# Values of a linear-attention head: projected with the tokens as the moving operand, turned by VectorE blocks and a pass through DRAM

## The chip, the cores and the metric

The kernel runs on one core of a Trainium2 chip. The metric is the device time in microseconds; the lower the better. A core has five engines that work from queues of their own and meet through semaphores: TensorE (PE, matmuls), VectorE (DVE), ScalarE (ACT), GpSimd (POOL) and SyncE (SP), which here issues nearly all transfers. TensorE reads SBUF and writes PSUM; of a matmul's two operands one stands still (the weights, loaded first) and one moves through (up to 512 columns). A transfer is issued on an engine's queue in order and then done by 16 shared DMA engines.

## The reference

One decoder layer for 2048 tokens of width 1024 in float32: a mixing stage, a gated MLP with a short convolution, and a final norm. Of the mixing stage the change touches the four heads of gated linear attention (HGRN2, key and value width 128) and the tiles that eight heads of windowed attention turn.

```python
u = rmsnorm(h, norm_mix_w)
hq, hf, hi, hg, att = split(u @ w_in, ...)
f = lb + (1 - lb) * sigmoid(hf);  k = 1 - f;  v = hi
# per head:  S_t = diag(f_t) S_{t-1} + k_t v_t^T,   o_t = S_t^T q_t
o_hg = rmsnorm(o) * silu(hg)
p = softmax(q k^T / 8 in a window of 128 keys, with a sink);  o_att = p @ v_att
h = h + concat(o_hg, o_att) @ w_out
h = h + (silu(conv(rmsnorm(h) @ w_gate)) * (rmsnorm(h) @ w_up)) @ w_down
out = rmsnorm(h)
```

## The kernel before

The tokens are done in two halves of 1024 (`hf`). Each half has a mixing stage, the output product (`out_proj`), the MLP (`gate_up`) and the down product (`down`), which also loads the next half's x and makes its first products.

All large products are float32 products split in two parts: an operand is a high part (rounded, `hi`) and the rest (`lo`), and each product is three matmuls, hi with hi, hi with lo, lo with hi. `prep` loads a weight tile of 128x1024 into a `raw` buffer (three of them, `RAW`), ScalarE casts it to `hi` and VectorE subtracts to get `lo` (two buffers each); the load is at line 198, the cast and the difference at 199 and 200. `unit` (line 203) then makes one product for 128 output rows and 1024 tokens: 8 pieces of the depth, three matmuls each, for two blocks of 512 tokens, so 48 matmuls. The weights stand and the tokens move, and the result has the features in the partitions and the tokens along them. It takes two PSUM banks of the pool `mm`, which has four.

The values of the linear heads are the exception. Their readers want the tokens in the partitions, so `project_v` (line 670) lets the tokens stand and the weights move: for a pair of heads and each of 8 groups of 128 tokens it makes 24 matmuls of 256 columns, and ScalarE scales the result by the tokens' inverse norms, which lie in the partitions (`rs`, line 685). `pu` (line 614) and `po` (line 634) read the values, in chunks of 128 tokens, as the moving operand. Two value tiles (`VB`) serve the four heads in turn.

A head goes through the stages f, q, l, s, p of the generator `hgrn`; a pair of attention heads through qa, sc, pv, pw of `attend`. `ORDER` (line 40) is the order in which these stages are written down, with v0 and v1 for the values of the two pairs, g for the gates and m for the splitting of the result. It gives each instruction a priority; a planner with its own model of the durations then lays out every engine's queue, so the blocks of one stage can lie inside those of another. What is laid out is fixed, and each engine works its queue in that order.

`turned` (line 335) turns a 128x1024 tile: VectorE transposes blocks of 32x32, and 16 transfers of 32 partitions x 1 KB, issued by SP, put the blocks in their places. It is used for the probabilities of three attention pairs in the sc stage (two tiles each, line 444) and for the outputs of three linear heads in the p stage (line 652), so 18 times in all. The tile between the two steps (`turn`) comes from the buffers `pp` or `t4`.

SP's queue carries the weights, x, the turns, and what passes through DRAM. GpSimd makes masks at the start and sets one half of `ST` to zero in the l stage of each head (line 507).

Of the kernel before, what the change touches and what calls it, by code (L numbers as in the profile page):

```python
# [17 lines left out]
P = 128  # L18
D = 1024
# [17 lines left out]
            ("P7", "S3", "T3"), ("P2", "A12", "B21"), ("P4", "A22", "T4")]  # L37
AFTER = {2: 'po'}
UP_AFTER = 'T2'
ORDER = ("f0 q0 l0 qa0 v0 sc0 s0 p0 f1 q1 pv0 pw0 l1 qa1 sc1 f2 s1 p1 q2 pv1 pw1 l2 qa2 v1 sc2 f3 s2 p2 q3 pv2 "  # L40
         "pw2 l3 qa3 sc3 s3 p3 pv3 pw3 g0 g1 m4 m5 m6 g2 m0 m1 g3 m7 m2 m3").split()
LEVELS = [1, 2, 4, 8, 16, 32, 64]
NEG = -1.0e30
UT = 7
# [1 line left out]
VB = 2  # L46
TURNED_PAIRS = 3
TURNED_HEADS = 3


@with_exitstack
def hymba_layer(ctx: ExitStack, tc: tile.TileContext, a: dict, out: bass.AP, rows_out: bass.AP):
# [139 lines left out]
    def prep(src, slots=False, parts=(slice(0, D),)):  # L192

        raw = raw4(None)
        hi, lo = [hp.tile([P, D], F32R, tag="m", name=f"w{t}", bufs=KT) if slots else
                  wp.tile([P, D], F32R, tag=t, name=f"w{t}", bufs=2) for t in ("hi", "lo")]
        for c in parts:
            nc.sync.dma_start(raw[:, c], src[:, c])
            nc.scalar.copy(hi[:, c], raw[:, c])  # L199
            nc.vector.tensor_tensor(lo[:, c], raw[:, c], hi[:, c].bitcast(F32), op=ALU.subtract)  # L200
        return hi, lo
# [130 lines left out]
        v = t[r, :]  # L332
        return bass.AP(v.tensor, v.offset + base, [list(v.ap[0])] + dims)

    def turned(p, tag, bufs, src, dst):

        t = p.tile([P, 4, 8, 32], F32, tag=tag, name="turn", bufs=bufs)
        nc.vector.transpose(t, src.rearrange("p n (c j) -> p c n j", j=32))
        for a in range(4):
            for c in range(4):  # L340
                nc.sync.dma_start(dst[32 * c:32 * c + 32, a], t[32 * a:32 * a + 32, c])

    def rows(kv):
        return slice(kv * HD, (kv + 1) * HD)
# [38 lines left out]
    def attend(hf, j, X, invb, KS, V, VD, mix, p):  # L383
# [9 lines left out]
        for g in range(NB):  # L393
            sc = p.tile([P, 2, 4, P], F32, tag="sc", name="sc", bufs=2)
            gs = slice(g * 512, (g + 1) * 512)
            for kv in range(2):
                r, other = rows(kv), rows(1 - kv)

                qx = p.tile([P, 2, 512], F32R, tag="pp", name="qx", bufs=3)
                qh, ql = qx[:, 0], qx[:, 1]  # L400
                nc.scalar.copy(qh[r], qT[r, gs])
                nc.scalar.copy(qh[other], qT[r, gs])
                nc.vector.tensor_tensor(ql[r], qT[r, gs], qh[r].bitcast(F32), op=ALU.subtract)
                nc.scalar.copy(ql[other], ql[r].bitcast(F32))
                for i0 in (0, 2):
                    pb = ps("at", "psc")
                    first = hf == 0 and g == 0 and i0 == 0
                    for i in range(2):
                        n = g * 4 + i0 + i
                        w0 = 1 if first and i == 0 else 0  # L410
                        o = pb[:, i * 256 + w0 * P:(i + 1) * 256]
                        ks = slice((n + w0) * P, (n + 2) * P)
                        for t, qx in enumerate((qh, ql)):
                            nc.tensor.matmul(o, qx[:, (i0 + i) * P:(i0 + i + 1) * P], KS[:, kv, ks],
                                             start=t == 0, stop=t == 1)
                    pv = pb.rearrange("p (i w k) -> p i w k", i=2, w=2)
                    dst = sc[:, kv, i0:i0 + 2]
                    if first:
                        nc.vector.memset(dst[:, 0], NEG)
                        nc.scalar.copy(dst[:, 1], pv[:, 1, 0])  # L420
                    else:
                        nc.scalar.copy(dst, pv[:, :, 0])
                    nc.vector.copy_predicated(
                        dst, C.own.bitcast(U32).unsqueeze(1).to_broadcast([P, 2, P]), pv[:, :, 1])
            m = p.tile([P, 2, 4], F32, tag="mx", name="m", bufs=2)
            nc.vector.tensor_reduce(m.rearrange("p a b -> p (a b)"),
                                    sc.rearrange("p a b c -> p (a b) c"), axis=AX.X, op=ALU.max)
# [12 lines left out]
            nc.vector.reciprocal(den, den)  # L440
            nc.vector.tensor_tensor(sc, sc, den.unsqueeze(3).to_broadcast([P, 2, 4, P]), op=ALU.mult)
            if j < TURNED_PAIRS:
                pt = p.tile([P, 4, 8, 32], F32, tag="sc", name="pt", bufs=2)
                turned(p, "pp", 3, sc.rearrange("p a b c -> p (a b) c"), pt)
                sc = pt
            scs.append(sc)
        yield
# [37 lines left out]
    def hgrn(hf, h, X, invb, vs, WG, gates, mix, p, fu=None):  # L485
# [112 lines left out]
        v = vs[h]  # L598

        kept = TT if hf + 1 < NH else TT - 1  # L600
        Kn = p.tile([P, TT, P], F32, tag="t4", name="Kn", bufs=2)
        for b in range(NB):
            pk = ps("hg", "pkn")
            n = min(4, kept - 4 * b)
            for i in range(n):
                c = slice((b * 4 + i) * P, (b * 4 + i + 1) * P)
                nc.tensor.transpose(pk[:, i * P:(i + 1) * P], K[:, c], ident)
            nc.scalar.copy(Kn[:, 4 * b:4 * b + n].rearrange("p a b -> p (a b)"), pk[:, 0:n * P])
        SS = p.tile([P, TT, P], F32, tag="SS", name="SS", bufs=1)
        for b in range(NB):  # L610
            pu = ps("hg", "pu")
            for c in range(4 * b, min(4 * b + 4, kept)):
                i = c % 4
                marks["pu"] = nc.tensor.matmul(pu[:, i * P:(i + 1) * P], Kn[:, c], v[:, c], start=True, stop=True)
            for c in range(4 * b, min(4 * b + 4, kept)):
                i = c % 4
                if hf == 0 and c == 0:
# [11 lines left out]
        for b in range(NB):  # L629
            at = [po[b][:, i * P:(i + 1) * P] for i in range(4)]  # L630
            empty = hf == 0 and b == 0
            for i in range(4):
                for k in range(2):
                    marks["po"] = nc.tensor.matmul(at[i][rows(k)], ST[:, k, 4 * b + i], v[:, 4 * b + i],
                                                   start=i == 0, stop=empty and i == 0, skip_group_check=True)
            for i in range(4):
                c = 4 * b + i
# [11 lines left out]
            mix[h] = g  # L649
        nc.vector.tensor_tensor(on, on, rs.unsqueeze(2).to_broadcast([P, TT, P]), op=ALU.mult)  # L650
        if h < TURNED_HEADS:
            turned(p, "t4", 2, on, q.rearrange("p (a c q) -> p a c q", a=4, c=TT))
        for b, bs in halves() if h >= TURNED_HEADS else ():
            pt = ps("hg", "pot")
            for i in range(4):
# [11 lines left out]
            nc.vector.tensor_copy(state[:, h], SS[:, TT - 1])  # L667
        yield

    def project_v(hf, pr, X, rs, p):  # L670

        v = [p.tile([P, TT, P], F32, tag="v", name="v", bufs=VB) for _ in range(2)]
        parts = [prep(a["w_v"][pr, s]) for s in range(2)]
        for tt in range(TT):
            o = ps("mm", "pvv")
            t = slice(tt * P, (tt + 1) * P)
            for kt in range(KT):
                hi, lo = parts[kt // 4]
                xh, xl = X[kt]
                c = slice((kt % 4) * 256, (kt % 4 + 1) * 256)  # L680
                nc.tensor.matmul(o[:, 0:256], xh[:, t], hi[:, c], start=kt == 0, stop=False)  # L681
                nc.tensor.matmul(o[:, 0:256], xl[:, t], hi[:, c], start=False, stop=False)  # L682
                nc.tensor.matmul(o[:, 0:256], xh[:, t], lo[:, c], start=False, stop=kt == KT - 1)  # L683
            for i in range(2):
                nc.scalar.activation(v[i][:, tt], o[:, i * P:(i + 1) * P], AF.Identity, scale=rs[:, tt:tt + 1])
        return v

    def split_into(h, l, src, eng=None):
# [465 lines left out]
    for hf in range(NH):  # L1154
        X, kv, invb, rs, f0 = nxt
        with ExitStack() as st:
# [7 lines left out]
            for name in ORDER:  # L1164
# [7 lines left out]
                elif stage == "w":  # L1172
                    WG[n] = prep(a["w_g"][n])
                elif stage == "v":
                    vs += project_v(hf, n, X, rs, p)
                else:
                    M[n] = split(mix[n], C.hgw if n < TURNED_HEADS else None)
            for n in (7, 3):
# [8 lines left out]
def _layout(i):  # L1187
# [3 lines left out]
    def cols(w, idx):  # L1191
# [10 lines left out]
    rows = [ar(P) + h * P for h in range(4)]  # L1202
    rows += [512 + np.concatenate([j * HD + ar(HD), (j + 4) * HD + ar(HD)]) for j in range(4)]
    w_out = i["w_out"][0][np.concatenate(rows)]
    w_v = np.stack([cols(w_in, 1024 + pr * 256 + ar(256)).reshape(P, 2, D).transpose(1, 0, 2) for pr in range(2)])
    conv = np.concatenate([i["conv_w"][0], i["conv_b"]], 0)
    d = {
        "xT": x.T.reshape(KT, P, S),
# [1 line left out]
        "norm_mix_w": i["norm_mix_w"][0].reshape(KT, P).T,  # L1210
        "w_q": np.stack([cols(w_in, h * P + ar(P)) for h in range(4)]),
        "w_f": np.stack([cols(w_in, 512 + h * P + ar(P)) for h in range(4)]),
        "w_v": w_v,
        "w_g": np.stack([cols(w_in, 1536 + h * P + ar(P)) for h in range(4)]),
        "w_att": np.stack([cols(w_in, c) for c in att]),
        "b_attn": np.stack([b[c - att0] for c in att], 1),
# [37 lines left out]
```

## Time and profile before

| | us |
|---|---|
| three runs, median (lowest to highest) | 2129.19 (2128.93 to 2129.20) |
| the profiled run | 2129.44 |
| its span, first to last instruction | 2127.7 |
| ScalarE busy | 1050.0 |
| GpSimd busy | 16.9 |

The span is the time from the first to the last instruction in the profile; what the profiled run has beyond it, 1.7 us, lies around it. The mixing stages take about 50 to 345 us and 1085 to 1400 us of the span; between them lie the output product, the MLP and the down product of the first half. Busy times are sums over the records of an engine. Matmuls are pipelined, and the ends of their records are modelled, so that the records of neighbours overlap.

### The profile page before, as it was taken

The numbers are of one execution on the slowest core, as the hardware profiler recorded it, in microseconds if no ns is written. First come the engines' busy times: TensorE is split into PE (matmuls) and PEld (weight loads), VectorE is DVE, ScalarE is ACT, GpSimd is POOL, SyncE is SP. The second block draws the span as 40 slices with busy tenths as digits, with TensorE's granted clock in tenths as the row PEclk, the third lists the DMA queues.
The fourth block names the chain that finished last, engine by engine and source line by source line (L and its number), as shares of the span: only waits on it lengthen the run. The fifth ranks groups of instructions, "written<-read, shape, count | busy, mean of one in ns | idle before, by whom it ended". The sixth has DMA issues, their size and how long they took to land.

```text
span 2127.7 us, 30275 instructions
## 1 busy us (share of the span) xinstructions
PE 2113.7 (99%) x11575; PEld 1763.0 (83%) x11575; DVE 1632.4 (77%) x2427; ACT 1050.0 (49%) x1855; POOL 16.9 (1%) x43
## 2 busy tenths in 40 slices
PE   8999999999999999999999999999999999999998
PEld 6988888888888888888889898888888888888887
DVE  6587786798887878785865776867988788887765
ACT  5455645564444445335635456555544444453353
POOL 2000000000000000000000000000000000000000
PEclk9999999999999999999999999999999999999999
DMA  4121213413232335964641212242223323259644
GB/s 162 42 59 45 68 52 102 136 59 121 91 124 92 98 116 168 379 235 150 216 143 40 61 38 64 60 146 97 80 99 103 110 90 124 94 194 403 228 149 134
DMA packets 105810, 264.34 MB, mean 124 GB/s; under 512 B 15808, under 2 KB 28608, under 8 KB 105664
## 3 DMA queue, kind: packets, MB, share of 16 engines
q1 hardware_dynamic: 105232, 262.14, 36.6%
q8 instruction: 91, 1.49, 0.3%
q14 instruction: 55, 0.45, 0.1%
q10 hardware_dynamic: 432, 0.27, 0.0%
HBM read 195.56 MB, written 57.34 MB: 119 GB/s over the span
## 4 chain that ended last, share of the span: by engine, by line
PE 97%; DVE 2%; DMA 1%; ACT 0%; issue 0%; SPq 0%; ACTq 0%; DVEq 0%
PE X L818 7%; PE X L816 7%; PE X L817 7%; PE pop L218 7%; PE hq L218 4%; PE q L218 4%; PE g L218 4%; PE f L218 4%; PE Y L817 4%; PE Y L818 4%; PE Y L816 4%; PE pdx L1004 3%; PE pdx L1003 3%; PE pdx L1005 3%; PE pdy L1004 3%; PE pdy L1003 3%
## 5 line engine op out<-in xcount | busy, mean ns | idle before, releaser
L689 ACT CAST whi<-raw 128x1024 fp32r<-128x1024 f32 x88 | 92.7, 1053 | 115.1 <-PE X L817 73.1
L816 PE MATMUL X<-T,whi 128*128 128x512 f32 x352 | 136.9, 389 | 0.0
L817 PE MATMUL X<-T,whi 128*128 128x512 f32 x352 | 136.9, 389 | 0.0
L818 PE MATMUL X<-T,wlo 128*128 128x512 f32 x352 | 136.9, 389 | 0.0
L887 DVE SCALAR_TENSOR_TENSOR y<-ga,cw,y 128x1024 f32<-128x1024 f32 x88 | 112.5, 1279 | 25.9 <-ACT y L885 25.9
L822 ACT COPY u<-X 128x512 f32<-128x512 f32 x88 | 51.5, 585 | 122.8 <-PE X L818 122.6
L690 DVE TENSOR_TENSOR wlo<-raw,whi 128x1024 fp32r<-128x1024 f32 x88 | 107.2, 1218 | 4.4 <-ACT whi L689 4.4
L199 ACT CAST whi<-raw 128x1024 fp32r<-128x1024 f32 x58 | 60.6, 1050 | 89.9 <-PE pop L218 36.7
L690 DVE TENSOR_TENSOR xld<-raw,xhd 128x1024 fp32r<-128x1024 f32 x72 | 80.9, 1131 | 18.3 <-ACT xhd L689 18.2
L689 ACT CAST xhd<-raw 128x1024 fp32r<-128x1024 f32 x72 | 70.0, 978 | 37.6 <-DMA raw<-act0T 12.0
L218 PE MATMUL pop<-XL,whi 128*128 128x512 f32 x256 | 82.8, 390 | 0.0
L218 PE MATMUL pop<-XH,wlo 128*128 128x512 f32 x256 | 82.6, 390 | 0.0
L218 PE MATMUL pop<-XH,whi 128*128 128x512 f32 x256 | 82.5, 391 | 0.0
L200 DVE TENSOR_TENSOR wlo<-raw,whi 128x1024 fp32r<-128x1024 f32 x58 | 70.5, 1217 | 10.4 <-ACT whi L199 10.1
L818 PEld LDWEIGHTS X<-T,wlo 128*128 128x128 f32 x352 | 66.1, 188 | 13.8
L817 PEld LDWEIGHTS X<-T,whi 128*128 128x128 f32 x352 | 66.1, 188 | 13.7
L816 PEld LDWEIGHTS X<-T,whi 128*128 128x128 f32 x352 | 66.0, 188 | 13.7
L682 PE MATMUL pvv<-whi,XL 128*128 128x256 f32 x256 | 72.7, 285 | 0.0
L681 PE MATMUL pvv<-whi,XH 128*128 128x256 f32 x256 | 72.6, 285 | 0.0
L683 PE MATMUL pvv<-wlo,XH 128*128 128x256 f32 x256 | 72.4, 287 | 0.0
L818 PE MATMUL X<-B,wlo 128*128 128x512 f32 x176 | 68.7, 390 | 0.8 <-DVE wlo L690 0.8
L817 PE MATMUL X<-T,Sh 128*128 128x512 f32 x176 | 68.6, 390 | 0.5 <-DVE T L690 0.5
(388 smaller groups left out, 6287.9 us busy)
## 6 DMA issues: line engine op xcount, KB each, us to landing
wr<-in_w_down SPq DMA_DIRECT2D x90, 512.0 KB, 5.6
raw<-in_w_gate SPq DMA_DIRECT2D x44, 512.0 KB, 3.6
raw<-in_w_up SPq DMA_DIRECT2D x44, 512.0 KB, 3.6
raw<-act0T SPq DMA_DIRECT2D x20, 512.0 KB, 5.6
raw<-act1T SPq DMA_DIRECT2D x20, 512.0 KB, 5.9
act0B<-y SPq DMA_DIRECT2D x33, 256.0 KB, 2.4
act1B<-y SPq DMA_DIRECT2D x33, 256.0 KB, 2.4
raw<-in_w_out SPq DMA_DIRECT2D x16, 512.0 KB, 3.7
```

The source lines that it names most:

```text
L218: nc.tensor.matmul(o[b], w, x[:, bs], start=f, stop=l)
L681: nc.tensor.matmul(o[:, 0:256], xh[:, t], hi[:, c], start=kt == 0, stop=False)
L682: nc.tensor.matmul(o[:, 0:256], xl[:, t], hi[:, c], start=False, stop=False)
L683: nc.tensor.matmul(o[:, 0:256], xh[:, t], lo[:, c], start=False, stop=kt == KT - 1)
L689: nc.scalar.copy(h, src)
L690: return (eng or nc.vector).tensor_tensor(l, src, h.bitcast(F32), op=ALU.subtract)
L816: nc.tensor.matmul(o, wh[:, ws], xh, start=i == 0 and not more, stop=False, skip_group_check=more)
L817: nc.tensor.matmul(o, wh[:, ws], xl, start=False, stop=False, skip_group_check=more)
L818: nc.tensor.matmul(o, wl[:, ws], xh, start=False, stop=i == 3, skip_group_check=more)
L887: nc.vector.scalar_tensor_tensor(y, g[:, w:w + HALF], C.cw[:, ft, w:w + 1], y, op0=ALU.mult, op1=ALU.add)
L1003: nc.tensor.matmul(o, wh[:, i, c], ah[:, i, cols], start=f, stop=False, skip_group_check=more)
L1004: nc.tensor.matmul(o, wh[:, i, c], al[:, i, cols], start=False, stop=False, skip_group_check=more)
```

## The change

Four edits, in one:

- The values are projected per head by `unit`, like every other product: weights stand, 512 tokens move, 48 matmuls. The weight layout is per head. The result, with the features in the partitions, is turned by `turned` into a value tile, and ScalarE scales it there, chunk by chunk. The stages v0 and v1 become v0 to v3, v0 and v1 where v0 was and v2 and v3 where v1 was.
- `turned` takes a list of sources, so that it can transpose two PSUM banks of 128x512. In place of 16 transfers from SBUF to SBUF there are five: one stores the tile of transposed blocks to DRAM (four tiles there, `DB`), and four load it back, each for 32 partitions. This holds for the 18 turns that there were and for the eight new ones.
- The value tile is laid out so that a chunk of 128 tokens' values is four runs of 32; `pu` and `po` read it so.
- `prep` issues its load on GpSimd's queue and not on SP's. That is 58 loads: all weights of the mixing stage and of the output product.

A branch for turning the keys in the same way is there too; with `TURNED_KEYS` at 0 it makes nothing.

```diff
-ORDER = ("f0 q0 l0 qa0 v0 sc0 s0 p0 f1 q1 pv0 pw0 l1 qa1 sc1 f2 s1 p1 q2 pv1 pw1 l2 qa2 v1 sc2 f3 s2 p2 q3 pv2 "
-         "pw2 l3 qa3 sc3 s3 p3 pv3 pw3 g0 g1 m4 m5 m6 g2 m0 m1 g3 m7 m2 m3").split()
+ORDER = ("f0 q0 l0 qa0 v0 v1 sc0 s0 p0 f1 q1 pv0 pw0 l1 qa1 sc1 f2 s1 p1 q2 pv1 pw1 l2 qa2 v2 v3 sc2 f3 s2 p2 q3 pv2 pw2 l3 qa3 sc3 s3 p3 pv3 pw3 g0 g1 m4 m5 m6 g2 m0 m1 g3 m7 m2 m3").split()
...
+TURNED_KEYS = 0
+DB = 4
...
         for c in parts:
-            nc.sync.dma_start(raw[:, c], src[:, c])
+            nc.gpsimd.dma_start(raw[:, c], src[:, c])
             nc.scalar.copy(hi[:, c], raw[:, c])
...
-    def turned(p, tag, bufs, src, dst):
+    def turned(p, tag, bufs, src, dst, strided=False):
 
         t = p.tile([P, 4, 8, 32], F32, tag=tag, name="turn", bufs=bufs)
-        nc.vector.transpose(t, src.rearrange("p n (c j) -> p c n j", j=32))
-        for a in range(4):
-            for c in range(4):
-                nc.sync.dma_start(dst[32 * c:32 * c + 32, a], t[32 * a:32 * a + 32, c])
+        tv = t.rearrange("p c n i -> p c (n i)").rearrange("p c (i n) -> p c n i", n=8) if strided else t
+        for i, s in enumerate(src):
+            n = 8 // len(src)
+            nc.vector.transpose(tv[:, :, i * n:(i + 1) * n], s.rearrange("p (n c j) -> p c n j", n=n, j=32))
+        d = dp.tile([P, 4, 256], F32, tag="turned", name="turned", bufs=DB)
+        nc.sync.dma_start(d.rearrange("p c x -> p (c x)"), flat(t))
+        for c in range(4):
+            nc.sync.dma_start(dst[32 * c:32 * c + 32].rearrange("p a b c -> p a (b c)"),
+                              d[:, c].rearrange("(a j) x -> j a x", a=4))
...
-                marks["pu"] = nc.tensor.matmul(pu[:, i * P:(i + 1) * P], Kn[:, c], v[:, c], start=True, stop=True)
+                marks["pu"] = nc.tensor.matmul(pu[:, i * P:(i + 1) * P], Kn[:, c], v[:, :, c], start=True, stop=True)
...
-    def project_v(hf, pr, X, rs, p):
-
-        v = [p.tile([P, TT, P], F32, tag="v", name="v", bufs=VB) for _ in range(2)]
-        parts = [prep(a["w_v"][pr, s]) for s in range(2)]
-        for tt in range(TT):
-            o = ps("mm", "pvv")
-            t = slice(tt * P, (tt + 1) * P)
-            for kt in range(KT):
-                hi, lo = parts[kt // 4]
-                xh, xl = X[kt]
-                c = slice((kt % 4) * 256, (kt % 4 + 1) * 256)
-                nc.tensor.matmul(o[:, 0:256], xh[:, t], hi[:, c], start=kt == 0, stop=False)
-                nc.tensor.matmul(o[:, 0:256], xl[:, t], hi[:, c], start=False, stop=False)
-                nc.tensor.matmul(o[:, 0:256], xh[:, t], lo[:, c], start=False, stop=kt == KT - 1)
-            for i in range(2):
-                nc.scalar.activation(v[i][:, tt], o[:, i * P:(i + 1) * P], AF.Identity, scale=rs[:, tt:tt + 1])
+    def project_v(h, X, rs, p):
+
+        o = unit(a["w_v"][h], X, "vT")
+        v = p.tile([P, 4, TT, 32], F32, tag="v", name="v", bufs=VB)
+        turned(p, "pp", 3, o, v)
+        for c in range(TT):
+            nc.scalar.activation(v[:, :, c], v[:, :, c], AF.Identity, scale=rs[:, c:c + 1])
         return v
...
-                    vs += project_v(hf, n, X, rs, p)
+                    vs.append(project_v(n, X, rs, p))
```

More of the change, by code (lines that the diff above doesn't have):

```diff
@@ L333, in across, with flat @@
         return bass.AP(v.tensor, v.offset + base, [list(v.ap[0])] + dims)
-    def turned(p, tag, bufs, src, dst):
+    def flat(t):
+        return t.rearrange("p a b c -> p (a b c)")
+    def turned(p, tag, bufs, src, dst, strided=False):
         t = p.tile([P, 4, 8, 32], F32, tag=tag, name="turn", bufs=bufs)
-        nc.vector.transpose(t, src.rearrange("p n (c j) -> p c n j", j=32))
-        for a in range(4):
-            for c in range(4):
-                nc.sync.dma_start(dst[32 * c:32 * c + 32, a], t[32 * a:32 * a + 32, c])
+        tv = t.rearrange("p c n i -> p c (n i)").rearrange("p c (i n) -> p c n i", n=8) if strided else t
[7 more added lines that the diff above has]
+                              d[:, c].rearrange("(a j) x -> j a x", a=4))
     def rows(kv):
@@ L443, in attend @@
                 pt = p.tile([P, 4, 8, 32], F32, tag="sc", name="pt", bufs=2)
-                turned(p, "pp", 3, sc.rearrange("p a b c -> p (a b) c"), pt)
+                turned(p, "pp", 3, [sc.rearrange("p a b c -> p (a b c)")], pt)
                 sc = pt
@@ L600, in hgrn @@
         kept = TT if hf + 1 < NH else TT - 1
-        Kn = p.tile([P, TT, P], F32, tag="t4", name="Kn", bufs=2)
-        for b in range(NB):
+        if h < TURNED_KEYS:
+            Kt = p.tile([P, 4, 32, TT], F32, tag="t4", name="Kt", bufs=2)
+            turned(p, "t4", 2, [K], Kt, True)
+            Kn = Kt.rearrange("p a i n -> p n (a i)")
+        else:
+            Kn = p.tile([P, TT, P], F32, tag="t4", name="Kn", bufs=2)
+        for b in range(NB) if h >= TURNED_KEYS else ():
             pk = ps("hg", "pkn")
@@ L633, in hgrn @@
                 for k in range(2):
-                    marks["po"] = nc.tensor.matmul(at[i][rows(k)], ST[:, k, 4 * b + i], v[:, 4 * b + i],
+                    marks["po"] = nc.tensor.matmul(at[i][rows(k)], ST[:, k, 4 * b + i], v[:, :, 4 * b + i],
                                                    start=i == 0, stop=empty and i == 0, skip_group_check=True)
@@ L651, in hgrn @@
         if h < TURNED_HEADS:
-            turned(p, "t4", 2, on, q.rearrange("p (a c q) -> p a c q", a=4, c=TT))
+            turned(p, "t4", 2, [on.rearrange("p c t -> p (c t)")], q.rearrange("p (a c q) -> p a c q", a=4, c=TT))
         for b, bs in halves() if h >= TURNED_HEADS else ():
@@ L1204, in _layout @@
     w_out = i["w_out"][0][np.concatenate(rows)]
-    w_v = np.stack([cols(w_in, 1024 + pr * 256 + ar(256)).reshape(P, 2, D).transpose(1, 0, 2) for pr in range(2)])
     conv = np.concatenate([i["conv_w"][0], i["conv_b"]], 0)
@@ L1212, in _layout @@
         "w_f": np.stack([cols(w_in, 512 + h * P + ar(P)) for h in range(4)]),
-        "w_v": w_v,
+        "w_v": np.stack([cols(w_in, 1024 + h * P + ar(P)) for h in range(4)]),
         "w_g": np.stack([cols(w_in, 1536 + h * P + ar(P)) for h in range(4)]),
```

## The prediction

> **What bounds the kernel now.** I read the page first, then the waits of TensorE, then TensorE's order of time. From the page (busy time and share, then the chain that ended last by engine):
>
> ```profile
> span 2127.7 us, 30275 instructions
> ...
> PE 2113.7 (99%) x11575; PEld 1763.0 (83%) x11575; DVE 1632.4 (77%) x2427; ACT 1050.0 (49%) x1855; POOL 16.9 (1%) x43
> ...
> PE 97%; DVE 2%; DMA 1%; ACT 0%; issue 0%; SPq 0%; ACTq 0%; DVEq 0%
> ```
>
> TensorE is busy for 2113.7 of 2127.7 us and carries 97% of the chain. What it still waits for is in its waits (total, times, longest) and in the windows (span, then busy time by engine):
>
> ```profile
> PE kv L218 <- ACT XH L232: 5.5, 1, 5.5
> ...
> 50.00:345.00 295.00, 295.00 (x2390) 252.50 (x2390) 220.70 (x414) 165.65 (x427) 0.52 (x1) 1.00 0.20 59
> 345.00:430.00 85.00, 85.00 (x402) 70.55 (x399) 55.26 (x91) 42.17 (x72) 0.00 (x0) 1.00 0.35 115
> 1085.00:1400.00 315.00, 315.00 (x2453) 268.68 (x2453) 228.54 (x418) 172.14 (x426) 2.09 (x4) 1.00 0.22 66
> ```
>
> The 5.5 us are the start. In the mixing stage of both halves (50 to 345 and 1085 to 1400 us), where the change lies, TensorE is busy without a gap and its clock is 1.00. VectorE is busy there for 75% and 73%. So a wait that ends elsewhere, a faster turn or a freer queue is worth nothing: only fewer or cheaper matmuls shorten this stage, and only a new gap on TensorE lengthens it.
>
> **The value products.** The groups by line (count, busy, mean ns) invite a wrong sum:
>
> ```profile
> L682 PE MATMUL pvv<-whi,XL 128*128 128x256 f32 x256 | 72.7, 285 | 0.0
> L218 PE MATMUL hq<-XL,whi 128*128 128x512 f32 x128 | 42.7, 393 | 0.0
> ```
>
> Three such groups make 768 matmuls of 256 columns; the change makes 384 of 512 columns of them (4 heads, 2 halves, 48 each), the form of hq. By the means that is 768 x 285 ns = 219 us against 384 x 393 ns = 151 us, a gain of 68. But a busy time is no cost here, since the records overlap. The cost is the distance from start to start, in TensorE's timeline:
>
> ```profile
> 79.02 0.39 PE L683 MATMUL pvv<-wlo,XH 128*128 128x256 f32 x1
> 79.24 0.28 PE L681 MATMUL pvv<-whi,XH 128*128 128x256 f32 x1
> ...
> 82.12 0.28 PE L681 MATMUL pvv<-whi,XH 128*128 128x256 f32 x1
> 82.33 0.39 PE L558 MATMUL plev<-Q,G 128*64 128x64 f32 x6
> ```
>
> ```profile
> 45.23 0.39 PE L218 MATMUL hq<-XH,wlo 128*128 128x512 f32 x1
> ...
> 50.69 0.39 PE L218 MATMUL hq<-XH,wlo 128*128 128x512 f32 x1
> ```
>
> From 79.24 to 82.12 lie 24 steps: 120 ns a matmul. From 45.23 to 50.69 lie 24 steps: 227.5 ns. Each pair of heads in each half therefore costs 192 x 0.120 = 23.04 us now and 96 x 0.2275 = 21.84 us after. The difference of 1.20 us arises four times: **-4.8 us**. It is one fourteenth of what the busy times promise.
>
> What two half-width matmuls cost more than one whole is 12.5 ns. The Trainium skill, TensorE: Matmul & The Clock Gate, section "Wait — 56ns, not 53.3ns?", puts a matmul of N columns at N / 2.4 GHz plus about 2.5 ns once the clock is up; by that the sum would be an estimated -1.0 us. The two measured distances differ from it, and I go by them.
>
> A second price stands in the same rows: where a block of other matmuls cuts into a run, the step into it is 0.21 us (82.12 to 82.33) and the step out 0.22 (79.02 to 79.24) instead of 0.12, some 0.2 us for each cut. The planner makes TensorE's order anew; ten cuts more or fewer in a half are 2 us. I take none, and keep both signs.
>
> The products that read the values (pu, po) now take them in four runs of 32 instead of 128 in a row. The trace has both kinds on one line:
>
> ```profile
> L471 PE MATMUL poT<-pt,V 128*64 128x128 f32 x180 | 17.9, 275 | 0.0
> L471 PE MATMUL poT<-pw,V 128*64 128x128 f32 x60 | 6.0, 278 | 0.0
> ```
>
> pt is read in such runs, pw in a row: no difference, so 0 us.
>
> **The new path of the values.** After each product come two VectorE block turns of 128x512 out of PSUM, one store to DRAM, a wait of SP for it, four loads, and eight scalings on ScalarE (eight per head before too). The trace has no turn out of PSUM and no such store and reload. The nearest rows:
>
> ```profile
> L338 DVE STREAM_TRANSPOSE turn<-sc x12: 1234/1239/1245, 116.1 to 1331.2; 128x1024 f32<-128x1024 f32 x12
> ...
> L741 DVE TENSOR_TENSOR h<-h,pop 128x512 f32<-128x512 f32 x16 | 10.3, 681 | 14.7 <-PE pop L218 14.7
> ...
> L685 ACT ACTIVATE v<-pvv,y x64: 344/360/369, 76.4 to 1277.6; 128x128 f32<-128x128 f32 x64
> ...
> keep<-h SPq DMA_DIRECT2D x32, 256.0 KB, 2.1
> h<-keep SPq DMA_DIRECT2D x16, 512.0 KB, 8.9
> ...
> act0T<-T SPq DMA_DIRECT2D x22, 256.0 KB, 3.1
> ...
> KS<-kcarry SPq DMA_DIRECT2D x1, 128.0 KB, 3.6
> ```
>
> A turn of half width is 0.62 (half of 1.239) to 0.68 us (L741 reads PSUM); I take 0.68, so 1.4 for two. VectorE gains 16 of them, 11 us in 610, under the TensorE stream that covers it at 75%. The store of 512 KB lies between 2.1 and 8.9; I take 3.1, the slowest store shown. Four issues are 4 x 0.63 = 2.5 (a sixteenth of the 10.08 us below, each), the last landing 1.8 to 3.6, taken at 3.6. Scaling is 8 x 0.36 = 2.9, as before. The chain is **13.5 us**, with ends 10.5 and 19.3. What covers it for head 0, whose values are wanted first:
>
> ```profile
> 97.01 0.28 PE L683 MATMUL pvv<-wlo,XH 128*128 128x256 f32 x1
> 97.13 1.10 PE L414 MATMUL psc<-KS,qx 128*128 128x128 f32 x8
> ...
> 103.98 0.38 PE L614 MATMUL pu<-v,Kn 128*128 128x128 f32 x2
> ...
> 188.31 0.28 PE L681 MATMUL pvv<-whi,XH 128*128 128x256 f32 x1
> ...
> 248.13 1.50 PE L614 MATMUL pu<-v,Kn 128*128 128x128 f32 x12
> ```
>
> After v0's last matmul TensorE has v1 (48 x 0.2275 = 10.9 us), then today's work from 97.0 to 104.0 (7.0): 17.9 us. So 0 us, with 4.4 to spare. Heads 1 to 3 have more: pvv of heads 2 and 3 starts at 188.3, and head 2's pu at 248.1.
>
> **The other turns.** Eighteen turns of probabilities and outputs lose 16 issues each for one store and four loads:
>
> ```profile
> 117.34 10.08 SPq L341 DMA_DIRECT2D pt<-turn  x16
> ...
> pt<-turn SPq DMA_DIRECT2D x192, 32.0 KB, 1.8
> ```
>
> Sixteen issues take 10.1 us, then 1.8 to land: 11.9. The new way is 3.1 + 2.5 + 3.6 = 9.2 (6.4 to 15.0). TensorE waits for none of them, so 0 us either way. SP now waits inside each turn for its store; behind it stand the next turn, the loads of h and the stores of keep, for which TensorE doesn't wait either.
>
> **The weight loads on GpSimd's queue.** 58 loads leave SP, where they waited long for their buffers and were stuck among turns:
>
> ```profile
> SPq L198 <- DVE wlo L200: 255.1, 31, 25.9
> ...
> 47.56 0.33 SPq L198 DMA_DIRECT2D raw<-in_w_f  x1
> ...
> 95.77 1.05 ACT L199 CAST whi<-raw 128x1024 fp32r<-128x1024 f32 x1 [0.69 <-PE pvv L682]
> ```
>
> A load issued at 47.6 is first touched at 95.8, and the cast waits for TensorE to free its buffer, not for the load. So 0 us. The trace has no load issued by GpSimd: between the 3.6 us of SP's w_f loads and 8.9 (h<-keep) I take the former, and 5 us more would vanish in that slack. Two joints remain. GpSimd's queue also holds the memsets of ST:
>
> ```profile
> POOL ST L507 <- DMA pt<-turn: 484.0, 2, 246.1
> ...
> 7.73 5.58 POOL L118 TENSOR_SCALAR_AFFINE_SELECT lmask<-lmask 128x64 f32<-128x64 f32 x10
> ...
> 19.39 0.33 SPq L198 DMA_DIRECT2D raw<-in_w_f  x1
> ...
> 2.00:4.00 2.00, 0.00 (x0) 0.00 (x0) 0.00 (x0) 0.73 (x2) 2.00 (x7) 1.00 0.93 267
> ...
> 10.00:12.00 2.00, 1.99 (x7) 1.09 (x6) 0.72 (x1) 1.91 (x3) 2.00 (x6) 1.00 1.02 412
> ```
>
> The memset that waits 246 us has nothing behind it now; after the change weights stand before and behind it, and lag only as far as the planner misjudges it. And at the start the DMA engines are full (share 0.93 to 1.02): if w_f goes out before the masks, at 13.3 us, and not at 19.4, its 512 KB at 267 to 412 GB/s put 1.3 to 2.0 us before the tiles of x. I take 0 for both.
>
> **Sum:** 2129.4 (the profiled run) - 4.8 = 2124.6; against the median of 2129.2, **2124.4 us**.
>
> **Rivals.**
> 1. The order gets smoother: 10 to 20 cuts fewer, 2 to 4 us: 2120.5 to 2122.5. For it: turns end sooner, so the small blocks come in one piece. Against: their number is the same.
> 2. The gain is given back at the joints: w_f in the first 16 us (2.0), more cuts (2 to 4), or a late weight. 2126.5 to 2133. This holds also the case that a column costs the same in both widths in the long run and nothing is saved: 2129.2, 4 in 100 by itself, against two plain rows. The clock page of the Trainium skill, weighed above, comes near that case.
> 3. Slower: head 0's values come late. SP takes turns one after another, and each now holds it for 3.1 + 2.5 = 5.6 us. With the store at its upper end and one other turn ahead the chain is 19.3 + 5.6 = 24.9 us; less 17.9, TensorE stands 7.0 us in each half: 2124.4 + 14.0 = 2138. It decides from a chain of 17.9 on, and is slower by 0.2% from 22.4. Against it: the nearest turn, pt at 117, follows the values by 20 us.
> 4. A load on GpSimd's queue is held while VectorE works, so that casts hold ScalarE up. With VectorE busy 75% a load of 3.6 us would take 14; three buffers then still give one in under 5 us, and a unit takes 10.9. Only a first load of a stage could be late, some 10 us in each half: 2144.
>
> The group of a VectorE operation with two inputs, beside the turn with one above:
>
> ```profile
> L200 DVE TENSOR_TENSOR wlo<-raw,whi 128x1024 fp32r<-128x1024 f32 x58 | 70.5, 1217 | 10.4 <-ACT whi L199 10.1
> ```
>
> The Trainium skill, SBUF — State Buffer, section "SBUF: two separate sides", warns of this hold for VectorE operations that use two ports for one stream. The trace doesn't show such a mode: 128x1024 takes 1.24 us with one input and 1.22 with two.
>
> **How the numbers follow.** Forecast 0.52 (2123 to 2126.5), rival 1 0.14, rival 2 0.22, rivals 3 and 4 together 0.12 (0.09 and 0.03). A measurement tells 0.2%, here 4.3 us, from no change; that line, 2124.9, runs through the forecast: 0.36 of it counts as faster, 0.16 as the same. Faster 0.36 + 0.14 = 0.50, same 0.16 + 0.22 = 0.38, slower 0.12. The range from 2120.5 to 2132 leaves out rivals 3 and 4 and the edge of 2.
>
> **What would show it.** Right: 384 vT matmuls at 227 ns from start to start, TensorE without a gap in both mixing stages, head 0's pu waiting for nothing. Wrong: a TensorE wait whose releaser is ScalarE's scaling of v or a turned tile (rival 3), a whi cast that waits for raw (rival 4), a start that reaches 16 us of kv work later (rival 2).

## The result

| | us |
|---|---|
| kernel before, four runs | 2129.19 (2128.93 to 2129.60) |
| changed kernel, four runs | 2142.76 (2140.80 to 2146.35) |
| ratio | 1.0065, 95% interval 1.0048 to 1.0083 |
| profiled run of the changed kernel, its span | 2143.43, 2141.7 |

The change makes the kernel 13.6 us slower, where 4.8 us faster was forecast; the time lies above the range. The page of the changed kernel (span; busy time by engine; the chain that ended last):

```profile
span 2141.7 us, 29401 instructions
...
PE 2115.2 (99%) x11191; PEld 1742.8 (81%) x11191; DVE 1639.2 (77%) x2443; ACT 1049.6 (49%) x1855; POOL 48.1 (2%) x101
...
PE 91%; DVE 4%; DMA 2%; ACT 1%; issue 1%; SPq 0%; DVEq 0%; ACTq 0%
```

TensorE's share of the chain falls from 97% to 91%: other engines now set its pace in places. Which, is in its waits (total, times, longest):

```profile
PE poT L481 <- DMA pt<-turned: 9.1, 4, 2.6
PE kv L219 <- ACT XH L233: 6.0, 2, 5.6
PE psc L424 <- DVE sc L433: 1.4, 1, 1.4
```

The second row is the start, as before. The first is new: matmuls that wait for probabilities on their way through DRAM. Among the signs of being wrong that the prediction lists, this one appeared, a TensorE wait for a turned tile; but the tile holds probabilities, not head 0's values. The windows over the two mixing stages, and over three of the places (span, then busy time by engine, TensorE's clock near the end):

```profile
50.00:345.00 295.00, 292.74 (x2176) 239.68 (x2174) 220.39 (x420) 163.74 (x417) 12.16 (x23) 1.00 0.29 89
1085.00:1400.00 315.00, 305.20 (x2195) 249.86 (x2195) 228.36 (x424) 168.87 (x422) 13.23 (x25) 0.99 0.29 87
...
220.00:225.00 5.00, 2.92 (x48) 2.38 (x44) 2.26 (x3) 0.58 (x1) 0.00 (x0) 1.00 0.74 151
...
1280.00:1285.00 5.00, 2.51 (x40) 2.06 (x42) 4.87 (x8) 0.71 (x2) 0.53 (x1) 0.82 0.77 238
1285.00:1290.00 5.00, 5.00 (x40) 4.37 (x37) 4.84 (x10) 1.72 (x3) 0.00 (x0) 0.84 1.06 296
1345.00:1350.00 5.00, 2.44 (x31) 1.81 (x30) 0.56 (x1) 1.82 (x3) 0.00 (x0) 1.00 0.87 255
1350.00:1355.00 5.00, 4.94 (x40) 3.84 (x42) 3.71 (x5) 1.23 (x2) 0.00 (x0) 0.66 0.38 108
```

Both stages were gapless at a clock of 1.00. Now TensorE stands for 2.3 and 9.8 us in them, and behind the second and third of the holes shown the clock is down (0.66 to 0.84); behind the first it stays at 1.00. The first place, in the timelines of VectorE and of SP (start, duration, what, and in brackets the idle time ahead and its releaser):

```profile
213.13 1.25 DVE L346 STREAM_TRANSPOSE turn<-sc 128x1024 f32<-128x1024 f32 x1
...
217.04 0.69 DVE L574 TENSOR_TENSOR K<-K,F 128x512 f32<-128x512 f32 x1
222.70 1.23 DVE L463 TENSOR_TENSOR po<-pt,ownT 128x1024 f32<-128x1024 f32 x1 [4.97 <-DMA pt<-turned]
```

```profile
214.40 1.01 SPq L348 DMA_DIRECT2D turned<-turn  x2
217.64 1.75 SPq L350 DMA_DIRECT2D pt<-turned  x4
```

The turn ends at 214.38, the store goes out at once, SP waits for it until 217.6, and the tile is there at 222.7, 8.3 us after the turn. But the reader of the tile, po<-pt, is laid out only 3.4 us of work behind the turn, so VectorE stands for 4.97 us with all its later work behind it.

The same turn and reader in VectorE's timeline of the kernel before:

```profile
208.57 1.24 DVE L338 STREAM_TRANSPOSE turn<-sc 128x1024 f32<-128x1024 f32 x1
...
222.35 1.23 DVE L453 TENSOR_TENSOR po<-pt,ownT 128x1024 f32<-128x1024 f32 x1
```

There 12.5 us lay between (222.35 less 209.81), and VectorE didn't wait for the tile. There are six places of this kind, the second block of 512 tokens of each turned pair (its second half, in what follows): without the wait for the tile, turn and reader lay 10.2 to 14.6 us apart before and lie 3.4 to 8.4 us apart now.

The second place, in the second half of the tokens, has a further side. In the timelines of TensorE and VectorE:

```profile
1277.02 0.61 PE L219 MATMUL vT<-XH,wlo 128*128 128x512 f32 x2
...
1282.89 0.49 PE L481 MATMUL poT<-pt,V 128*64 128x128 f32 x4 [1.94 <-DMA pt<-turned]
...
1287.27 0.50 PE L219 MATMUL f<-XH,whi 128*128 128x512 f32 x1
```

```profile
1285.60 2.51 DVE L346 STREAM_TRANSPOSE turn<-vT 128x512 f32<-128x512 f32 x4
```

The wait is again for pt. But between the last product of v3 (1277.6) and the first of head 3's f lie 9.6 us in which no large product fills such waits, and TensorE is idle for 2.7 us in all. f takes the banks of the values, and these are turned only from 1285.6 on. In the first half of the tokens f follows v3 at once.

### The profile page after: what moved, and what is told of

The parts are those of the page before. It is cut to its first block, busy times and chain, and to the rows that moved or that the text cites. A ratio compares the mean times of both kernels' runs of the same rounds, so it can differ in the third digit from the quotient of the medians.

```text
span 2141.7 us, 29401 instructions
## 1 busy us (share of the span) xinstructions
PE 2115.2 (99%) x11191; PEld 1742.8 (81%) x11191; DVE 1639.2 (77%) x2443; ACT 1049.6 (49%) x1855; POOL 48.1 (2%) x101
## 4 chain that ended last, share of the span: by engine, by line
PE 91%; DVE 4%; DMA 2%; ACT 1%; issue 1%; SPq 0%; DVEq 0%; ACTq 0%
PE pop L219 7%; PE X L824 7%; PE X L823 7%; PE X L822 7%; PE hq L219 4%; PE g L219 4%; PE Y L824 4%; PE Y L823 4%; PE Y L822 4%; PE q L219 4%; PE pdx L1011 3%; PE pdx L1010 3%; PE pdx L1009 3%; PE f L219 3%; PE pdy L1010 3%; PE pdy L1011 3%
## 5 line engine op out<-in xcount | busy, mean ns | idle before, releaser
L433 DVE COPY_PREDICATED sc<-own,psc 128x256 f32<-128x256 uint32 x64 | 27.5, 448 | 55.3 <-ACT sc L432 42.3
L823 PE MATMUL X<-T,Sh 128*128 128x512 f32 x176 | 68.6, 390 | 0.6 <-DVE T L696 0.6
L822 PE MATMUL X<-B,whi 128*128 128x512 f32 x176 | 68.7, 390 | 0.0
L822 PE MATMUL X<-T,Sh 128*128 128x512 f32 x176 | 68.7, 390 | 0.0
```

Of the source, the lines that this page charges most:

```text
L822: nc.tensor.matmul(o, wh[:, ws], xh, start=i == 0 and not more, stop=False, skip_group_check=more)
L823: nc.tensor.matmul(o, wh[:, ws], xl, start=False, stop=False, skip_group_check=more)
```

## The experiments

Eighteen kernels. In the tables, "time" is the median, and the ratio is to the kernel before in the same session (2129.1 to 2129.4).

### Taking the change apart

| kernel | what it is | time | ratio, 95% |
|---|---|---|---|
| undo_dram | changed kernel, all 26 turns by 16 transfers | 2151.90 | 1.0106 (1.0091 to 1.0121) |
| undo_queue | changed kernel, weight loads on SP's queue | 2137.08 | 1.0038 (1.0026 to 1.0051) |
| only_dram | kernel before, its 18 turns through DRAM | 2133.23 | 1.0018 (1.0009 to 1.0028) |
| only_values | kernel before, values by the new product, turned by 16 transfers | 2150.33 | 1.0099 (1.0084 to 1.0114) |

undo_dram puts the old transfers back into `turned`; only_dram does the reverse in the kernel before; only_values takes `project_v`, `ORDER` and the readers from the change, with this loop; undo_queue moves the weight loads back to SP's queue, where only_values has them too:

```diff
-        d = dp.tile([P, 4, 256], F32, tag="turned", name="turned", bufs=DB)
-        nc.sync.dma_start(d.rearrange("p c x -> p (c x)"), flat(t))
-        for c in range(4):
-            nc.sync.dma_start(...)
+        for a in range(4):
+            for c in range(4):
+                nc.sync.dma_start(dst[32 * c:32 * c + 32, a], t[32 * a:32 * a + 32, c])
...
-            nc.gpsimd.dma_start(raw[:, c], src[:, c])
+            nc.sync.dma_start(raw[:, c], src[:, c])
```

> The changed kernel with all 26 turns done by 16 transfers inside SBUF again; values by 512-column products and weights on GpSimd's queue stay. Theory A (the store and reload is the loss: TensorE and VectorE are laid out to read a turned tile sooner than its 8.3 us are over): the loss goes and the 4.8 us of the products show, 2123 to 2127 us. Theory B (the new path of the values is the loss, however they are turned): 2138 to 2146. Theory C (GpSimd's queue is the loss): 2138 to 2146.

> The changed kernel with the weight loads on SP's queue again; all else stays. Theory A: 2140 to 2146 us, perhaps some more, since the weights stand among the turns again. Theory B: 2138 to 2146. Theory C: 2123 to 2128.

> The kernel before with one edit: its 18 turns pass through DRAM. Values and weight queue are as before. Theory A: most of the 18.4 us between the sum (2124.4) and the measurement (2142.8) shows, 2138 to 2148 us, with TensorE waiting for pt tiles. Theory B and theory C: 2128 to 2131.

> The kernel before with one edit: values by 512-column products, turned by 16 transfers; weights on SP's queue. Theory A: 2123 to 2127 us, the gain of the products alone. Theory B: 2138 to 2146. Theory C: 2123 to 2128. SP then issues 128 transfers of 0.63 us more than before, 80 us in all, so that weights behind them can be late: up to 2132 under any theory.

Theory A, that the way through DRAM is the loss, falls: without it the kernel is 9 us slower still, and alone it costs 3.9. C, that the queue is the loss, explains 5.7 of the 13.6 us. The values cost most (B): 21 us with the old transfers. Each of the four times lies outside the range of the theory that it comes nearest to, so the theories had the direction at best, not the size. The profile of only_values shows where. Its windows, from the end of the products of v3 to the start of head 3's f:

```profile
220.00:225.00 5.00, 3.87 (x50) 2.91 (x49) 4.91 (x9) 1.63 (x2) 0.00 (x0) 1.00 0.40 132
225.00:230.00 5.00, 1.82 (x48) 1.55 (x48) 3.52 (x7) 1.46 (x4) 0.00 (x0) 0.71 0.20 48
230.00:235.00 5.00, 3.93 (x24) 3.19 (x26) 2.55 (x4) 1.17 (x2) 0.00 (x0) 0.50 0.44 125
235.00:240.00 5.00, 5.00 (x33) 4.16 (x30) 1.87 (x3) 2.34 (x4) 0.00 (x0) 0.77 0.17 40
```

TensorE is idle for 5.4 us of the first 15, and its clock falls to 0.50. In that stretch it has only small blocks until f starts, and of its five waits four end with VectorE.

### The values: banks, work or order

| kernel | what it is | time | ratio, 95% |
|---|---|---|---|
| no_turn | only_values without the turn of the values: ScalarE scales them straight from PSUM, so that their readers get them untransposed | 2129.51 | 1.0002 (0.9992 to 1.0011) |
| f_turn | changed kernel, the values' turn tile in the buffers of f instead of pp | 2140.02 | 1.0050 (1.0035 to 1.0065) |
| v3_later | changed kernel, v3 behind f3 in `ORDER` | 2143.95 | 1.0064 (1.0047 to 1.0081) |
| only_queue | kernel before, weight loads on GpSimd's queue | 2129.39 | 1.0000 (0.9991 to 1.0009) |

The edits of f_turn, v3_later and no_turn, in this order:

```diff
-        turned(p, "pp", 3, o, v)
+        turned(p, "f", 2, o, v)
...
-... qa2 v2 v3 sc2 f3 s2 ...
+... qa2 v2 sc2 f3 v3 s2 ...
...
-            nc.scalar.activation(v[:, :, c], v[:, :, c], AF.Identity, scale=rs[:, c:c + 1])
+            nc.scalar.activation(v[:, :, c], oc, AF.Identity, scale=rs[:, c:c + 1])
```

> The kernel with the values alone changed (512-column products, SP's weight queue, 16-transfer turns elsewhere), and the turn of the values left out: ScalarE scales them straight out of PSUM into the value tile, so that the values aren't transposed. Theory B1 (the loss is that v2's and v3's four PSUM banks are held until VectorE turns them, which waits for a turn buffer, so that head 3's f can't begin): the banks are free at once and the products' gain is all that is left, 2123 to 2126 us. Theory B3 (the 512-column products aren't cheaper as they lie in this kernel): 2129 us or more. Theory B2 (the turn of the values costs through the work it gives VectorE and SP, wherever that lies): 2123 to 2126 too.

> The changed kernel with one word altered: the values' turn tile takes a buffer of tag f (two of the same size) and not one of pp, which the probabilities hold. Theory B1: the turn of v2 and v3 no longer waits for the probabilities, the gap after them shrinks, 2128 to 2138 us; f buffers are used by head 3's f, so some of the wait may come back there. Theory B2: 2140 to 2146, as the changed kernel.

> The changed kernel with v3 written after f3 in the order, and not behind v2. Theory B1: v2 and f3 have a pair of banks each, TensorE has wide products while the turns run, 2128 to 2137 us. Theory B2: 2140 to 2146, since the same work is done on VectorE and SP.

> The kernel before with one edit: the weight loads on GpSimd's queue. With the changed kernel the queue was worth +5.7 us (2142.8 against 2137.1). Theory C1 (loads issued by GpSimd cost by themselves, by a later landing or a busier memory): 2133 to 2136 us. Theory C2 (they cost only through another order of the work around the late turns): 2128 to 2131.

The queue alone costs nothing. Without the turn 20.8 us go, so the loss hangs on the turn, not on the product. no_turn is still no faster than the kernel before, which is what B3 (the products aren't cheaper as they lie here) expected. But its windows have 3.7 us of holes at 345 to 360 us, where poT waits 1.9 us for pw and po 1.4 for m, and a clock of 0.66 in the last 5 of these; so this run can't tell B3 from a gain that another place gave back. By their times f_turn and v3_later speak for B2. f_turn's trace says more: v2 is turned within 1 and 5 us of the end of its product, the hole between v3 and f is gone in both halves of the tokens, and the kernel is 2.7 us faster than the changed one; yet other holes remain (3.4 and 6.7 us of idle TensorE in the two stages). So the buffer has a part, and not the largest in this kernel.

### The reader of the probabilities

| kernel | what it is | time | ratio, 95% |
|---|---|---|---|
| g1_16 | changed kernel, turns of each pair's second half by 16 transfers | 2144.16 | 1.0071 (1.0056 to 1.0086) |
| g1_16_sp | the same, weight loads on SP's queue | 2144.80 | 1.0072 (1.0055 to 1.0088) |
| dram_for_v_sp | kernel before, values by the new product and through DRAM, other turns by 16 transfers | 2145.58 | 1.0076 (1.0061 to 1.0091) |
| dram_queue | kernel before, 18 turns through DRAM, weight loads on GpSimd's queue | 2134.88 | 1.0027 (1.0017 to 1.0037) |

```diff
-                turned(p, "pp", 3, [sc.rearrange("p a b c -> p (a b c)")], pt)
+                turned(p, "pp", 3, [sc.rearrange("p a b c -> p (a b c)")], pt, direct=g == 1)
```

> The changed kernel, but the turns of the second half of each attention pair's probabilities (6 of the 26 turns) go from SBUF to SBUF by 16 transfers again. Theory L: the loss comes from the one reader that stands closest behind its turn. In the kernel before VectorE's product po<-pt of a pair's second half started 11.5 to 14.6 us after the end of its turn (10.2 to 14.6 of them filled with laid-out work); in the changed kernel only 3.4 to 8.4 us of work are laid between, and the data takes 7.3 to 11.0 us, so VectorE stands 15.0 us in 4 places and TensorE 9.1 us behind it, with its clock down afterwards. Then with 16 transfers the work between is back at 10 us or more, TensorE's waits for a turned pt fall from 9.1 to under 1 us, and the time falls from 2142.8 to 2129 to 2134. Theory M: the eight new turns of the values load VectorE's and SP's queues and their PSUM banks are held, whichever way other turns go: 2138 or more, with other waits of TensorE in place of those for pt.

> As the run before, with the weight loads on SP's queue again. Theory L: the queue matters only through where the reader of pt comes to stand; with that taken away both queues give the same within 2 us: 2128 to 2134. Theory M: 2135 or more (the changed kernel with SP's queue took 2137.1).

> The kernel before with the values by the new product and turned through DRAM; the 18 other turns by 16 transfers, the weights on SP's queue. Theory L: no wait for pt, so the gain of the products (4.8 us by the distance from start to start) shows, less some small joints: 2125 to 2130. Theory M: the values' new path costs by itself, 2135 or more; with the values turned by 16 transfers it was 2150.3.

> The kernel before with the 18 turns through DRAM and the weights on GpSimd's queue, the values as before. Turns through DRAM alone took 2133.2, the queue alone 2129.4. Theory L: the same wait for pt as with the DRAM turns alone, shifted by where the planner lays it: 2131 to 2136. If the queue by itself makes transfers through DRAM later (it added 5.7 us beside the values): 2138 to 2140.

This theory, L, falls as the only cause. In g1_16 turn and reader lie 9.5 us or more apart again, its TensorE waits for a turn of probabilities no longer than 0.8 us, and it is no faster: the holes are in another place. Between v3's products and f its TensorE is idle for 5.5 us in each half of the tokens, where the changed kernel has none and 2.7. dram_for_v_sp shows that place bare, in TensorE's timeline and in VectorE's:

```profile
219.15 0.62 PE L219 MATMUL vT<-XH,wlo 128*128 128x512 f32 x2
...
221.27 0.64 PE L573 MATMUL plev<-Q,G 128*64 128x64 f32 x16
225.16 0.69 PE L573 MATMUL plev<-Q,G 128*64 128x64 f32 x16 [3.25 <-DVE Q L580]
227.39 1.12 PE L573 MATMUL plev<-Q,G 128*64 128x64 f32 x16 [1.55 <-DVE Q L580]
...
232.68 0.51 PE L219 MATMUL f<-XH,whi 128*128 128x512 f32 x1
```

```profile
228.21 1.23 DVE L468 TENSOR_TENSOR po<-pt,ownT 128x1024 f32<-128x1024 f32 x1
229.47 2.51 DVE L346 STREAM_TRANSPOSE turn<-vT 128x512 f32<-128x512 f32 x4
```

The last product of v3 ends near 219.8, and then no large product runs for 13 us. The four vT tiles, all four banks of `mm`, are turned at 229.5 to 232.0, both heads in one go and right behind the pair's second po; f follows at 232.68, when a bank is free. VectorE wasn't waiting there: the turns were laid out that late. They need a buffer of `pp`, which has three, for the pair's qx, turn, po and pw as well.

### The turn without a buffer of pp

| kernel | what it is | time | ratio, 95% |
|---|---|---|---|
| own_v | changed kernel, values turned from PSUM into the value tile itself, stored and loaded back into it | 2140.17 | 1.0050 (1.0037 to 1.0062) |
| own_v_sp | the same, weight loads on SP's queue | 2129.47 | 1.0000 (0.9991 to 1.0009) |
| own_v_16 | dram_for_v_sp with the same edit | 2125.01 | 0.9983 (0.9974 to 0.9992) |

```diff
-    def turned(p, tag, bufs, src, dst, strided=False):
+    def turned(p, tag, bufs, src, dst, strided=False, t=None):
-        t = p.tile([P, 4, 8, 32], F32, tag=tag, name="turn", bufs=bufs)
+        if t is None:
+            t = p.tile([P, 4, 8, 32], F32, tag=tag, name="turn", bufs=bufs)
...
-        turned(p, "pp", 3, o, v)
+        turned(p, "pp", 3, o, v, t=v)
```

> The changed kernel, but VectorE turns vT from PSUM into the value tile itself, which is stored to DRAM and loaded back into itself, so that the turn needs no buffer of pp. Same products, same VectorE, ScalarE and SP work. B1 (banks of vT held until a pp buffer is free): VectorE turns v2 within some us of its last product, head 3's f follows v3's product without a hole, the holes at 220 to 235 and 1280 to 1297 us go, and the time falls from 2142.8 to 2125 to 2133, what is left being waits for a turned pt. B2 (the work itself costs): 2139 or more.

> The same with the weight loads on SP's queue. B1: 2125 to 2132 (from 2137.1). B2: 2135 or more.

> The kernel before with the values by the new product, turned into the value tile itself and through DRAM; the 18 other turns by 16 transfers, weights on SP's queue (with the buffer of pp it took 2145.6). B1: the gain of the products shows, 2124 to 2129, under the kernel before. B2: 2140 or more.

Between dram_for_v_sp and own_v_16 only the place of one tile differs; products, turns, transfers and scalings are the same, and **20.6 us** go. own_v_16 is 4.4 us faster than the kernel before. The same stretch in its timelines of VectorE and TensorE:

```profile
208.83 1.31 DVE L347 STREAM_TRANSPOSE v<-vT 128x512 f32<-128x512 f32 x2
...
222.75 1.31 DVE L347 STREAM_TRANSPOSE v<-vT 128x512 f32<-128x512 f32 x2
```

```profile
70.72 0.40 PE L219 MATMUL vT<-XL,whi 128*128 128x512 f32 x1
...
75.05 0.61 PE L219 MATMUL vT<-XH,wlo 128*128 128x512 f32 x2
...
219.79 0.62 PE L219 MATMUL vT<-XH,wlo 128*128 128x512 f32 x2
220.25 0.61 PE L219 MATMUL f<-XH,whi 128*128 128x512 f32 x2
```

v2 is turned at 208.8, 20 us earlier; its banks are free when v3's product ends, and f follows in the next step. B1 (banks held because the turn waits for a buffer) is shown for this pair of kernels, as far as the timelines can: the hole of 5.3 us in each half goes with the one buffer. The wait for the buffer is not itself in a trace: VectorE doesn't stand there, its turns are laid out late. B2 (the work costs) falls, since the work is the same, and B3 with it, since the same products now gain. own_v misses its 2125 to 2133: the hole is gone there too, as in f_turn, and only 2.6 us are gained.

### The queue in company

| kernel | what it is | time | ratio, 95% |
|---|---|---|---|
| own_v_16_q | own_v_16, weight loads on GpSimd's queue | 2124.11 | 0.9977 (0.9968 to 0.9986) |
| own_v_pt | the same, the 12 turns of probabilities through DRAM too | 2128.74 | 1.0000 (0.9991 to 1.0010) |
| own_v_on | own_v_16_q, the 6 turns of outputs through DRAM too | 2126.79 | 0.9991 (0.9981 to 1.0000) |

```diff
-        if tag == "pp" and len(src) == 2:
+        if tag == "pp":
...
-        if tag == "pp" and len(src) == 2:
+        if tag != "pp" or len(src) == 2:
```

> own_v_16 (2125.0) with the weight loads on GpSimd's queue. Theory Q1: the queue does harm only where readers of tiles that the shorter turns bring are laid close behind them; here only the values' tiles are such, so 2124 to 2128. Theory Q2: with the loads off SP's queue the whole order is laid out tighter, and ScalarE stands for the values' tiles with the scores behind it (in own_v 46.3 us, 7 times, VectorE 7.7 us at a time behind it): 2133 to 2140, with TensorE waiting for VectorE's sc and K.

> own_v_16_q with the 12 turns of probabilities through DRAM as well, the 6 of outputs by 16 transfers. Theory P: the reader of the turned probabilities, laid 3 to 8 us behind the turn where the way takes 7 to 11, is what costs: 2135 to 2141, near own_v. Theory O (the outputs' turns, or all together): 2124 to 2130.

> own_v_16_q with the 6 turns of outputs through DRAM as well, the 12 of probabilities by 16 transfers. Theory P: 2123 to 2128, no wait for a turned tile on TensorE. Theory O: 2133 or more.

own_v_16_q is the fastest kernel of the study, 5.3 us under the one before. On GpSimd's queue the probabilities' turns add 4.6 us and the outputs' 2.7, but both together, own_v, 16.1. Neither theory foresaw that. One of own_v's holes, in the timelines of ScalarE, VectorE and TensorE, shows its form:

```profile
1291.72 2.45 ACT L692 ACTIVATE v<-v,y 128x128 f32<-128x128 f32 x8 [9.08 <-DMA v<-turned]
1294.08 0.35 ACT L433 COPY sc<-psc 128x256 f32<-128x256 f32 x1
1297.55 2.45 ACT L692 ACTIVATE v<-v,y 128x128 f32<-128x128 f32 x8 [3.11 <-DMA v<-turned]
1299.90 0.35 ACT L433 COPY sc<-psc 128x256 f32<-128x256 f32 x1
```

```profile
1294.46 0.45 DVE L434 COPY_PREDICATED sc<-own,psc 128x256 f32<-128x256 uint32 x1 [7.66 <-ACT sc L433]
...
1300.28 0.45 DVE L434 COPY_PREDICATED sc<-own,psc 128x256 f32<-128x256 uint32 x1 [3.99 <-ACT sc L433]
```

```profile
1303.94 0.69 PE L583 MATMUL plev<-Q,K 128*64 128x64 f32 x16 [1.78 <-DVE K L587]
```

ScalarE stands for the values' tiles, the score copies lie behind the scalings, VectorE stands for the copies, TensorE for VectorE. But ScalarE stands for values about as long in own_v_sp (52.8 us) as in own_v (46.3), and there TensorE waits neither for VectorE's scores nor for K. What differs is the order laid out, which the queue of the loads shifts. Why it comes out so badly in this one combination stays open.

## Why the prediction was wrong

**Where the 13.6 us come from.** One way through the runs, one edit at a time: kernel before 2129.4; own_v_16 2125.0 (-4.4, the new products with a turn that holds nothing up); own_v_sp 2129.5 (+4.5, the other 18 turns through DRAM); undo_queue 2137.1 (+7.6, the values' turn tile in `pp`); changed kernel 2142.8 (+5.7, the queue). The steps depend on what else is there (us; the values pass through DRAM in all seven kernels):

| turn tile of the values | other 18 turns | loads on SP | loads on GpSimd |
|---|---|---|---|
| in `pp` | 16 transfers | 2145.6 | not run |
| in `pp` | through DRAM | 2137.1 | 2142.8, the change |
| in the value tile | 16 transfers | 2125.0 | 2124.1 |
| in the value tile | through DRAM | 2129.5 | 2140.2 |

The turn tile in `pp` costs 20.6, 7.6 or 2.6 us. The other turns through DRAM save 8.5 us where the tile is in `pp`, and cost 4.5 or 16.1 where the turn goes into the value tile. The queue costs from -0.9 to 10.7. Out of the changed kernel the queue alone gives back 5.7 us and the tile alone 2.6, but both together 13.3 (own_v_sp). So no single part is the cause of the 13.6.

**What failed in the prediction.** Its one gain held. The failure is in the terms that it put at 0: the values' new path, the other turns and the queue. Each was held against the readers and the slack of the old order. The order is made anew, and in it they lie elsewhere: pt's turn and reader, 10.2 to 14.6 us apart before, are 3.4 to 8.4 apart now. The three follow below.

**The value products** (step of -4.8 us): right. In own_v_16's rows above vT takes 19 steps from 70.72 to 75.05, 228 ns each, and the kernel is 4.4 us faster, own_v_16_q 5.3. That the first comes so near to 4.8 is in part luck, since TensorE is idle for 2.9 us in own_v_16's two stages and not at all in those of the kernel before. The estimate of -1.0 by the page of the Trainium skill, TensorE: Matmul & The Clock Gate, section "Wait — 56ns, not 53.3ns?", is outside both intervals (-5.5 to -1.7 and -6.8 to -3.0 us, by the ratios); the measured distances decide.

**The reads in runs of 32**: no cost shows; pu takes 275 ns in the mean as before.

**The new path of the values** (0 us): the first step that failed. Its length was right: head 0's turn starts at 83.15, ScalarE's scaling in the changed kernel is

```profile
93.51 2.46 ACT L691 ACTIVATE v<-v,y 128x128 f32<-128x128 f32 x8 [11.58 <-DMA v<-turned]
```

and ends at 95.97: 12.8 us against 13.5 estimated, and TensorE covers it, as said. What was wrong is the sentence that followed: "Heads 1 to 3 have more: pvv of heads 2 and 3 starts at 188.3, and head 2's pu at 248.1." It costs the path by its last reader alone. The path also holds things while it runs. The old product drained each bank after 24 matmuls by two scalings on ScalarE straight into the value tiles; the new one fills all four banks with v2 and v3, and they come free only when VectorE turns them, which needs a buffer of `pp` amid the pair's scores. The one that was late is no reader of the values, but head 3's f, the next user of the banks. With the other turns as before this costs 20.6 us; in the changed kernel, where the hole is in the second half of the tokens alone, 2.6. Rival 3 had the sign, but not the place (head 0) or the thing (the landing).

**The other turns** ("TensorE waits for none of them, so 0 us either way"): the second step that failed, by 3.9 us alone (only_dram; 5.7 with GpSimd's queue, dram_queue) and by -8.5 to 16.1 with the rest of the change. The way was sized right, 7.3 to 11.0 us in the four places where VectorE waited for it, against 9.2. But the reader had been laid out to fit the 12 us of the old way; with five issues in place of 16 it is laid out closer, and the shorter way is still longer than the new distance. VectorE's waits for pt go from 5.1 us in 3 places to 15.0 in 4, and TensorE's from none to 9.1, the longest of its new waits in the changed kernel. With these gone (g1_16) the banks' hole was longer instead, so the 9.1 us are no price either. "A faster turn is worth nothing" held; that it can cost was not asked.

**The weight loads on GpSimd's queue** (0 us): right alone (2129.39) and in own_v_16_q. That "lag only as far as the planner misjudges it" would be the whole price was the soft spot: in company it is 5.7 us, the third step that failed, and how it comes about stays open. Rival 4 didn't occur: the loads land in 4.0 to 4.4 us (medians of the weights, only_queue) against 3.6 to 3.9 from SP, and in the changed kernel no cast of line 200 waits for one. Nor did the start get longer: TensorE's wait there is 6.0 us against 5.5, and the first matmuls of hq come 0.7 us sooner.

**The estimates by nearest rows** came near, by the medians: the turn out of PSUM 0.70 us (0.68 taken), the store 2.9 (3.1), the four issues 1.8 (2.5), the last landing 3.6 over all turns and 4.1 for the values (3.6).

## What to carry to other kernels

When a step moves from an engine that drains PSUM at once to a longer path, cost it at the next user of what it holds (banks, buffers), not at its last reader. Where the order is laid out ahead by a model, a shorter transfer can draw its reader closer; check the new distance against the measured way, since an in-order engine that stands takes all its later work along. And put a staging tile into a buffer that lies idle anyway, here the destination itself: that one line decided 20.6 us in one combination of edits. In another it decided 2.6, so try an edit in more than one.

## What was not expected of the hardware

A hole can cost more than its length. In only_values, summed over windows of 5 us from 30 to 1500 us, TensorE is idle for 16 us, and its clock takes another 8 (busy time times the clock's shortfall); in the kernel before the two are 1.5 and 0. The clock fell to 0.50 although the waits of 1.2 to 1.7 us at 225 to 235 us lay between blocks of small matmuls: a stretch mostly idle sufficed. Not every hole does it: in the changed kernel the clock stays at 1.00 behind waits of 2.1 us (ended at 222.8) and 2.5 us (1216.3), and falls behind one of 1.9 us (1282.9). Windows around that one:

```profile
1282.00:1283.10 1.10, 0.20 (x4) 0.23 (x4) 1.10 (x3) 0.00 (x0) 0.49 (x1) 1.00 0.76 309
1283.20:1286.50 3.30, 3.02 (x37) 2.76 (x36) 3.21 (x6) 0.00 (x0) 0.00 (x0) 0.50 0.79 216
1286.60:1290.00 3.40, 3.40 (x26) 2.77 (x23) 3.31 (x7) 1.72 (x3) 0.00 (x0) 1.00 1.08 300
```

The stretch at 0.50 lasts some 3.4 us here, 6.8 in dram_for_v_sp (225.9 to 232.7) and 10.2 in only_values (227.1 to 237.3), once, twice and three times the same length. The Trainium skill, TensorE: Matmul & The Clock Gate, section "Part 1: The HAM clock gate", gives half rate after an idle window of about 3.4 us, and full rate after as long a busy one; the 0.50 agrees with the first, and the stretches of 3.4 us and its multiples agree with a window of that length. How busy TensorE must be in a window to keep the clock, no run here shows.
